# Weight low parts by a ScalarE pass and an accumulating DMA, in place of a GpSimd subtraction

## The chip, the cores and the metric

The kernel runs on one NeuronCore of a Trainium2 chip. The metric is the device time of one execution in microseconds. A core has five engines that run side by side and wait for each other by semaphores: TensorE (PE, matrix products), VectorE (DVE), ScalarE (ACT), GpSimd (POOL) and SyncE (SP, which here only issues transfers). The transfers of all queues run on the core's 16 DMA engines.

## The reference

A two-layer encoder over 256 frames of 2048 channels, in float32. Every sub-layer is `x <- x + norm_post(f(norm_pre(x)))` with root-mean-square norms. Layer 0's mixer projects the input to 3072 columns, pools one third over windows of 2 to 16 frames, sends the rest through a gate, a causal depthwise convolution of width 31, a layer norm and a swish, and projects back; layer 1's mixer is `y = W_out(B * conv3(C * h))` with B, C, h from one projection. Each mixer is followed by a dense MLP:

```python
def sq_relu_mlp(h, w1, w2):
    a = jax.nn.relu(jnp.einsum("btd,df->btf", h, w1))
    return jnp.einsum("btf,fd->btd", a * a, w2)
```

Nearly all of the arithmetic is products of the 256 frames with weight matrices that are read once.

## The kernel before, in words

**Products in three terms.** TensorE multiplies in a rounded float32 type (`F32R`). To keep float32's precision both factors are split in a high part (the value rounded) and a low part (the value minus its high part), and each product is made as high x high, high x low and low x high: L216, L217 and L218 in `mms`. The activations (`xh`/`xl`, `ah`/`al`, `yh`/`yl`) are the stationary factor and the weights (`whi`/`wlo`) the moving one; 256 frames are two row blocks `t`.

**The weight stream.** `specs` lists 722 weight slices in the order of their use, each 256 rows by 512 columns, in SBUF a tile of 128 partitions x 1024 numbers (512 KB). `prep_to(i)` (L166) prepares them up to slice i: SyncE loads the slice to a `raw` tile (L170), ScalarE rounds it to `whi` (L173), and an engine subtracts `whi` from `raw` to give `wlo` (L174). There are four `raw` buffers and nine of `whi` and of `wlo`. A load waits until the readers of the slice four before are done with their raw buffer; a rounding waits until TensorE is done with the slice nine before. `ahead` asks for slices up to eight beyond those that a block of products needs.

**Who subtracts.** VectorE does it for 633 slices. GpSimd does it for 89: the 62 slices 8 to 69 (from `lo_eng[0] = lambda i: pool` at L471 to L595, the stretch in which VectorE works through 31 x 8 convolution taps at L383 and L385), and nine slices at the start of each of `f1_0_0_0`, `sC0` and `f1_1_0_0` (L159 to L161), which are used right after a sub-layer ends.

**Boundaries of sub-layers.** `mix_close` (L558) forms the row scale of the sub-layer just done: ScalarE's square sums (L555 or L669) and root (L565), then VectorE's short chain L564, L289, L291, L292, L293 on one column per row. `close_row` adds the scaled block to the residual `x` (L319, 128x512 pieces). TensorE transposes `x` (L245), ScalarE rounds the transposed block (L231) and VectorE makes its low part (L234); only then can the next sub-layer's products start. Row scales of the pre-norm (L276, L287) follow later, since they are applied to the results.

**What sets the order.** Each engine executes its own list in order. The lists are made at build time by a scheduler that simulates the engines, so a change of one instruction can move others by some places.

Of the kernel before, what the change touches and what calls it, by code (L numbers as in the profile page):

```python
# [10 lines left out]
F32 = mybir.dt.float32  # L11
F32R = mybir.dt.float32r
BF16 = mybir.dt.bfloat16
AF = mybir.ActivationFunctionType
ALU = mybir.AluOpType
# [18 lines left out]
def trunk_kernel(  # L34
# [7 lines left out]
    pe, act, dve, pool = nc.tensor, nc.scalar, nc.vector, nc.gpsimd  # L42
# [14 lines left out]
    def nm(s):  # L57
        uid[0] += 1
        return f"{s}_{uid[0]}"

    def t512(shape=(P, CB), dt=F32):
        return tp.tile(list(shape), dt, tag="t512", name=nm("t"))

    def small(n=1):
        return sp.tile([P, n], F32, tag="sm", name=nm("sm"), padded_shape=[P, 4])
# [4 lines left out]
    def pst():  # L70
        return ps_t.tile([P, CB], F32, tag="t", name=nm("pt"))

# [1 line left out]
    xs = [cst.tile([P, D], F32, tag=f"x{t}", name=f"x{t}") for t in range(NT)]  # L74

    def load_x(t, c):
# [10 lines left out]
    par = cst.tile([P, 96 + 48 + 248], F32, tag="par", name="par")  # L87
    offs = {}

    def par_load(keyed, col, eng=pool):  # L90
        """Rows of 128 channels, one DMA per source, to be transposed to columns of par."""
        rows = t512()[:, :P]
        n = 0
        for key, v in keyed:
            offs.setdefault(key, col + n)
            eng.dma_start(rows[n : n + v.shape[0], :], v)
            n += v.shape[0]

        def tr():
            p = pst()  # L100
            pe.transpose(p[:, :n], rows[:n, :], ident[:n, :n])
            act.copy(par[:, col : col + n], p[:, :n])

        return tr
# [5 lines left out]
        o = offs[key] + i  # L110
        return par[:, o : o + 1]

# [1 line left out]
    specs = []  # L114

    def add_seg(w, k0, nk, c0):
# [42 lines left out]
    pool_lo = set()  # L159
# [3 lines left out]
    nxt = [0]  # L163
    lo_eng = [lambda i: dve]

    def prep_to(i):  # L166
        while nxt[0] <= min(i, len(specs) - 1):
            src, nj = specs[nxt[0]]
            raw = wp.tile([P, 2 * CB], F32, tag="raw", name=nm("raw"), bufs=4)
            nc.sync.dma_start(raw.rearrange("p (j n) -> p j n", j=nj), src)  # L170
            hi = wp.tile([P, 2 * CB], F32R, tag="whi", name=nm("whi"))
            lo = wp.tile([P, 2 * CB], F32R, tag="wlo", name=nm("wlo"))
            act.copy(hi, raw)  # L173
            (pool if nxt[0] in pool_lo else lo_eng[0](nxt[0])).tensor_tensor(lo, raw, hi.bitcast(F32), ALU.subtract)  # L174
            wt[nxt[0]] = (hi, lo)
            nxt[0] += 1

# [9 lines left out]
    tasks = []  # L187

    def later(d, fn):
        """Emit fn after d more slices of matrix products."""  # L190
        tasks.append([d, fn])

    def tick():
# [28 lines left out]
        n = len(ids)  # L222
        prep_to(ids[-1] + (AHEAD // 2 if t == 0 else AHEAD))

# [1 line left out]
    def split_cols(p, col0, dst, scale_cols):  # L226
        """PSUM bank of 4 transposed [128, 128] blocks, each times its column -> hi, lo."""
        hi, lo = dst
        for j in range(4):
            pj = p[:, j * P : (j + 1) * P]  # L230
            act.activation(hi[:, col0 + j, :], pj, AF.Copy, scale=scale_cols[j])  # L231
        for j in range(4):
            pj = p[:, j * P : (j + 1) * P]
            dve.scalar_tensor_tensor(  # L234
                lo[:, col0 + j, :], pj, scale_cols[j], hi[:, col0 + j, :].bitcast(F32),
                ALU.mult, ALU.subtract,
            )

    def split_plain(src, hi, lo):
        act.copy(hi, src)  # L240
        dve.tensor_tensor(lo, src, hi.bitcast(F32), ALU.subtract)  # L241
# [7 lines left out]
    def new_xT(t):  # L249
        for h in range(2):  # L250
            xT[t, h] = (
                xp.tile([P, 8, P], F32R, tag="xh", name=nm("xh")),
                xp.tile([P, 8, P], F32R, tag="xl", name=nm("xl")),
            )
# [7 lines left out]
    def norm_chunk(t, c, gkey, gbase):  # L262
        p = pst()
        transpose4(xs[t][:, c * CB : (c + 1) * CB], p)
        split_cols(p, 4 * (c % 2), xT[t, c // 2], [pcol(gkey, gbase + 4 * c + j) for j in range(4)])

    def sumsq(parts):
        s = small()
        dve.tensor_reduce(s, parts, mybir.AxisListType.X, ALU.add)
        return s  # L270
# [11 lines left out]
    def rsqrt(v, y=None, root=None):  # L282
        s = small()
        if root:
            root(s)
        else:
            act.activation(s, v, AF.Sqrt)  # L287
        y = y or small()
        dve.reciprocal(y, s)  # L289
        h = small()  # L290
        dve.scalar_tensor_tensor(h, y, v, y, ALU.mult, ALU.mult)  # L291
        dve.tensor_scalar(h, h, -0.5, 1.5, ALU.mult, ALU.add)  # L292
        dve.tensor_tensor(y, y, h, ALU.mult)  # L293
        return y
# [10 lines left out]
        return g  # L305

    def close_row(t, s, nxt_gain, final=False):
        """x += s * m, then the next sub-layer's transposed, gained, split input."""
        if not final:
            new_xT(t)  # L310
        for c in range(4):
            cs = slice(c * CB, (c + 1) * CB)
            if final and c == 0:
                for q in (slice(0, CB // 2), slice(CB // 2, CB)):
                    dve.scalar_tensor_tensor(xs[t][:, q], ms[t][:, q], s, xs[t][:, q],
                                             ALU.mult, ALU.add)
                    nc.sync.dma_start(out[t * P : (t + 1) * P, q], xs[t][:, q])
                continue
            dve.scalar_tensor_tensor(xs[t][:, cs], ms[t][:, cs], s, xs[t][:, cs], ALU.mult, ALU.add)  # L319
            if final:  # L320
                nc.sync.dma_start(out[t * P : (t + 1) * P, cs], xs[t][:, cs])
            else:
                later(2 + (c + 1) // 2, lambda c=c: norm_chunk(t, c, *nxt_gain))

# [1 line left out]
    for t in range(NT):  # L326
        new_xT(t)
    first = par_load((("mix_pre", chan_rows(mix_pre_g)),), 0, act)
# [37 lines left out]
    for i, tr in enumerate(rest):  # L366
        later(1 + i, tr)
# [42 lines left out]
            pwin.append(w)  # L410

    def pool_sum(g):
        """Windowed sums over time minus count times the frame, then / count."""
        ic = t512((P, T))
        nc.sync.dma_start(ic, inv_cnt[g * T : (g + 1) * T].partition_broadcast(P))
        p = pst()
        for c in range(2):
            ct = 2 * g + c
            o = p[:, c * T : (c + 1) * T]
            n = 0  # L420
            for s in range(2):
                for m in (uh[s], ul[s]):
                    pe.matmul(o, m[:, ct * P : (ct + 1) * P], pwin[s][:, g * T : (g + 1) * T],
                              start=n == 0, stop=n == 3)
                    n += 1
        pd = t512((P, 2, T))
        dve.tensor_tensor(
            pd, p.rearrange("p (c n) -> p c n", c=2),
            ic.unsqueeze(1).to_broadcast([P, 2, T]), ALU.mult,
        )  # L430
        ph = tp.tile([P, 2, T], F32R, tag="ph", name=nm("ph"), bufs=2)
        pl = tp.tile([P, 2, T], F32R, tag="pl", name=nm("pl"), bufs=2)
        split_plain(pd, ph, pl)
        pd_[g] = (ph, pl)
# [114 lines left out]
            split_plain(z, hi[:, :, tsl], lo[:, :, tsl])  # L549

    def mix_evac(t, cb, ps, gp, parts):
        """Mixer output block: square sums, and the block times the post-norm gain."""
        junk = tp.tile([P, CB], BF16, tag="junk", name=nm("junk"), bufs=2)
        i = nparts[t] = nparts.get(t, -1) + 1
        act.activation(junk, ps, AF.Square, accum_out=parts[t][:, i % 4 : i % 4 + 1])  # L555
        dve.tensor_tensor(ms[t][:, cb * CB : (cb + 1) * CB], ps, gp, ALU.mult)  # L556

    def mix_close(t, parts, nxt_gain, final=False):  # L558
        """Last block's square sum joins the others' on the way into the root."""
        base = small()  # L560
        dve.tensor_scalar(base, sumsq(parts[t][:, :3]), 1.0 / D, EPS, ALU.mult, ALU.add)
        last = parts[t][:, 3:4]
        v = small()
        dve.scalar_tensor_tensor(v, last, 1.0 / D, base, ALU.mult, ALU.add)  # L564
        r = rsqrt(v, root=lambda s: act.activation(s, last, AF.Sqrt, bias=base, scale=1.0 / D))  # L565
        close_row(t, r, nxt_gain, final)
# [47 lines left out]
        if cb == 1:  # L614
            mix_close(t, parts, ("ffn_pre", 0))

# [1 line left out]
    def ffn(l, nxt_gain, final=False):  # L618
        for t in range(NT):
            later(3 + t, lambda t=t: row_scale(t))  # L620
# [53 lines left out]

    ffn(0, ("mix_pre", KT))

# [1 line left out]
    for t in range(NT):  # L678
        later(3 + t, lambda t=t: row_scale(t))

# [107 lines left out]
```

## Time and profile before

| | |
|---|---|
| median of 3 runs | 2093.64 us (2092.41 to 2095.49) |
| the profiled execution: span from the first to the last instruction | 2096.0 us |
| busy: TensorE, VectorE, ScalarE, GpSimd | 2048.8, 1187.4, 1007.8, 221.5 us |
| of GpSimd's: the 89 subtractions | 214.3 us, 2.435 us each |
| VectorE's 633 subtractions | 775.4 us, 1.227 us each |
| ScalarE's 722 roundings | 760.1 us, 1.054 us each |
| transfers | 390.31 MB, 186 GB/s over the span |

The span is the profiled execution's own time as far as the profile gives it; what lies around it isn't shown. In the profile's lines a group reads: line, engine, operation, destination<-sources with shapes, count | busy us, mean ns of one | idle time of the engine just before, and what ended it. A wait reads: who <- whom: us in all, times, longest. Timelines give start and duration in us, and in brackets the idle time before.

### The profile page before, as it was taken

The numbers are of one execution on the slowest core, as the hardware profiler recorded it, in microseconds if no ns is written. First come the engines' busy times: TensorE is split into PE (matmuls) and PEld (weight loads), VectorE is DVE, ScalarE is ACT, GpSimd is POOL, SyncE is SP. The second block draws the span as 40 slices with busy tenths as digits, with TensorE's granted clock in tenths as the row PEclk, the third lists the DMA queues.
The fourth block names the chain that finished last, engine by engine and source line by source line (L and its number), as shares of the span: only waits on it lengthen the run. The fifth ranks groups of instructions, "written<-read, shape, count | busy, mean of one in ns | idle before, by whom it ended". The sixth has DMA issues, their size and how long they took to land.

```text
span 2096.0 us, 24559 instructions
## 1 busy us (share of the span) xinstructions
PE 2048.8 (98%) x9253; PEld 1693.0 (81%) x9253; DVE 1187.4 (57%) x1494; ACT 1007.8 (48%) x1296; POOL 221.5 (11%) x111
## 2 busy tenths in 40 slices
PE   8999889999999999999999999989999999999998
PEld 7888778888888888887788888878888888888886
DVE  4787765445454555546655655565455454454545
ACT  7454565445344354444643444465444444354443
POOL 5886210000000000002100000220000000000000
PEclk9999999999999999999999999999999999999999
DMA  7665445556565555555555565546556565565553
GB/s 259 197 208 174 151 161 191 190 171 206 196 196 171 196 186 196 189 173 170 174 199 180 182 204 181 191 156 212 180 178 211 174 201 186 175 202 199 192 170 120
DMA packets 203079, 390.31 MB, mean 186 GB/s; under 512 B 12368, under 2 KB 14512, under 8 KB 202960
## 3 DMA queue, kind: packets, MB, share of 16 engines
q1 hardware_dynamic: 202656, 388.55, 56.3%
q8 instruction: 72, 1.18, 0.2%
q14 instruction: 47, 0.39, 0.1%
q0 software_dynamic: 256, 0.18, 0.0%
q10 hardware_dynamic: 48, 0.02, 0.0%
HBM read 386.60 MB, written 2.10 MB: 185 GB/s over the span
## 4 chain that ended last, share of the span: by engine, by line
PE 84%; DVE 3%; DMA 1%; ACT 0%; issue 0%; DVEq 0%; SPq 0%; ACTq 0%
PE pg L218 27%; PE pg L216 27%; PE pg L217 27%; PE pt L245 2%; DVE x L319 1%; DVE sm L291 0%; DVE sm L293 0%; DMA gp<-in_mix_post_g_dram 0%; DMA raw<-in_ab_w_out_dram 0%; DVE sm L564 0%; DMA raw<-in_ffn_w_dram 0%; DMA raw<-in_sc_w_in_dram 0%; DVE m L556 0%; ACT whi L173 0%; DVE m L671 0%
## 5 line engine op out<-in xcount | busy, mean ns | idle before, releaser
L174 DVE TENSOR_TENSOR wlo<-raw,whi 128x1024 fp32r<-128x1024 f32 x633 | 775.4, 1227 | 583.9 <-ACT whi L173 550.3
L173 ACT CAST whi<-raw 128x1024 fp32r<-128x1024 f32 x722 | 760.1, 1054 | 581.8 <-PE pg L218 381.8
L218 PE MATMUL pg<-whi,xl 128*128 128x512 f32 x1568 | 618.5, 395 | 17.9 <-DVE xl L234 17.9
L216 PE MATMUL pg<-whi,xh 128*128 128x512 f32 x1568 | 612.6, 392 | 1.3 <-ACT xh L231 0.7
L217 PE MATMUL pg<-wlo,xh 128*128 128x512 f32 x1568 | 612.2, 391 | 0.0
L217 PE MATMUL pg<-wlo,ah 128*128 128x512 f32 x1024 | 399.2, 390 | 0.0
L216 PE MATMUL pg<-whi,ah 128*128 128x512 f32 x1024 | 398.7, 389 | 0.0
L218 PE MATMUL pg<-whi,al 128*128 128x512 f32 x1024 | 398.2, 391 | 0.0
L218 PEld LDWEIGHTS pg<-whi,xl 128*128 128x128 f32 x1568 | 295.8, 189 | 79.0 <-DVE xl L234 20.1
L217 PEld LDWEIGHTS pg<-wlo,xh 128*128 128x128 f32 x1568 | 295.8, 189 | 61.7
L216 PEld LDWEIGHTS pg<-whi,xh 128*128 128x128 f32 x1568 | 295.9, 189 | 61.1 <-ACT xh L231 1.7
L174 POOL TENSOR_TENSOR wlo<-raw,whi 128x1024 fp32r<-128x1024 f32 x89 | 214.3, 2435 | 1012.4 <-DVE wlo L174 693.8
L217 PEld LDWEIGHTS pg<-wlo,ah 128*128 128x128 f32 x1024 | 192.6, 188 | 40.2
L216 PEld LDWEIGHTS pg<-whi,ah 128*128 128x128 f32 x1024 | 192.6, 188 | 39.5
L218 PEld LDWEIGHTS pg<-whi,al 128*128 128x128 f32 x1024 | 192.5, 188 | 39.3
L634 ACT ACTIVATE t<-pg,rr 128x512 f32<-128x512 f32 x64 | 43.8, 685 | 190.6 <-PE pg L218 190.6
L664 DVE TENSOR_TENSOR m<-pg,m 128x512 f32<-128x512 f32 x112 | 76.9, 686 | 89.4 <-PE pg L218 89.4
L216 PE MATMUL pg<-whi,yh 128*128 128x512 f32 x256 | 101.2, 396 | 1.6 <-ACT yh L240 1.5
L217 PE MATMUL pg<-wlo,yh 128*128 128x512 f32 x256 | 100.9, 394 | 0.0
L218 PE MATMUL pg<-whi,yl 128*128 128x512 f32 x256 | 98.8, 391 | 0.2 <-DVE yl L241 0.2
L385 DVE SCALAR_TENSOR_TENSOR acc<-pp,par,acc 128x256 f32<-128x256 f32 x240 | 96.3, 479 | 0.1
L241 DVE TENSOR_TENSOR al<-pt,ah 128x512 fp32r<-128x512 f32 x64 | 44.0, 687 | 71.8 <-ACT ah L240 71.7
(124 smaller groups left out, 858.8 us busy)
## 6 DMA issues: line engine op xcount, KB each, us to landing
raw<-in_ffn_w_dram SPq DMA_DIRECT2D x512, 512.0 KB, 4.7
raw<-in_sc_w_in_dram SPq DMA_DIRECT2D x96, 512.0 KB, 4.8
raw<-in_ab_w_in_dram SPq DMA_DIRECT2D x48, 512.0 KB, 4.4
raw<-in_ab_w_out_dram SPq DMA_DIRECT2D x32, 512.0 KB, 3.9
raw<-in_sc_w_out_dram SPq DMA_DIRECT2D x32, 512.0 KB, 5.4
x<-in_x_dram SPq DMA_DIRECT2D x8, 256.0 KB, 7.7
gp<-in_mix_post_g_dram SPq DMA_DIRECT2D x8, 256.0 KB, 6.2
gp<-in_ffn_post_g_dram SPq DMA_DIRECT2D x8, 256.0 KB, 4.3
```

The lines of the kernel that those rows point to most:

```text
L173: act.copy(hi, raw)
L174: (pool if nxt[0] in pool_lo else lo_eng[0](nxt[0])).tensor_tensor(lo, raw, hi.bitcast(F32), ALU.subtract)
L216: pe.matmul(ps, lh, wh, start=start and k == 0, stop=False)
L217: pe.matmul(ps, lh, wl, start=False, stop=False)
L218: pe.matmul(ps, ll, wh, start=False, stop=stop and k == n - 1)
L241: dve.tensor_tensor(lo, src, hi.bitcast(F32), ALU.subtract)
L245: pe.transpose(p[:, j * P : (j + 1) * P], src[:, j * P : (j + 1) * P], ident)
L319: dve.scalar_tensor_tensor(xs[t][:, cs], ms[t][:, cs], s, xs[t][:, cs], ALU.mult, ALU.add)
L385: dve.scalar_tensor_tensor(a, src, wcol, a, ALU.mult, ALU.add)
L634: act.activation(rl, ps, AF.Relu, scale=rr[t])
L664: dve.tensor_tensor(dst, ps, dst, ALU.add)
```

## The change

For the 89 slices that GpSimd subtracted, ScalarE makes a second pass over the raw tile, `Copy` with the factor -1 into the `F32R` tile `wlo`, which gives minus the rounded weights; then GpSimd's queue issues a transfer that adds the raw tile to `wlo` in place (`accum_op`). The result is raw minus rounded, as before. TensorE's low-part products now wait for that transfer, and so does the load that reuses the raw buffer. The slices that VectorE subtracts are as they were. The change also empties some comment lines; all lines after L174 stand five lower in the new file.

```diff
             act.copy(hi, raw)
-            (pool if nxt[0] in pool_lo else lo_eng[0](nxt[0])).tensor_tensor(lo, raw, hi.bitcast(F32), ALU.subtract)
+            eng = pool if nxt[0] in pool_lo else lo_eng[0](nxt[0])
+            if eng is pool:
+                act.activation(lo, raw, AF.Copy, scale=-1.0)
+                pool.dma_start(lo, raw, accum_op=ALU.add)
+            else:
+                eng.tensor_tensor(lo, raw, hi.bitcast(F32), ALU.subtract)
             wt[nxt[0]] = (hi, lo)
```

ScalarE's list where the long GpSimd stretch begins (slices 8 and on), before and then after. Numbers in names count tiles and differ between the two.

```order
L231 ACTIVATE xh_99<-pt_306,par 128x128 x4
L173 CAST whi_427<-raw_425 128x1024
L173 CAST whi_433<-raw_431 128x1024
L173 CAST whi_439<-raw_437 128x1024
L231 ACTIVATE xh_103<-pt_319,par 128x128 x4
L173 CAST whi_445<-raw_443 128x1024
L102 COPY par<-pt_510 128x64
```
```order
L236 ACTIVATE xh_99<-pt_306,par 128x128 x4
L173 CAST whi_427<-raw_425 128x1024
L176 ACTIVATE wlo_428<-raw_425 128x1024
L173 CAST whi_434<-raw_432 128x1024
L176 ACTIVATE wlo_435<-raw_432 128x1024
L173 CAST whi_441<-raw_439 128x1024
L176 ACTIVATE wlo_442<-raw_439 128x1024
L236 ACTIVATE xh_103<-pt_319,par 128x128 x4
L173 CAST whi_448<-raw_446 128x1024
L176 ACTIVATE wlo_449<-raw_446 128x1024
L102 COPY par<-pt_522 128x64
```

Behind each rounding stands the second pass over the same raw tile, and the other work of ScalarE behind both.

SyncE's loads in the same stretch with the semaphores they wait for, before and then after. `Pool` is GpSimd, `Activation` ScalarE, `DMASW` a transfer that GpSimd issued, `DMAHW` one of SyncE's own.

```order
L170 DMA raw_455<-in_ab_w_in_dram 128x2x512 [waits DMAHW4_49,Pool_49]
L170 DMA raw_461<-in_ab_w_in_dram 128x2x512 [waits DMAHW5_49,Pool_49]
L170 DMA raw_467<-in_ab_w_in_dram 128x2x512 [waits DMAHW6_49,Pool_49]
L170 DMA raw_473<-in_ab_w_in_dram 128x2x512 [waits DMAHW7_49,Pool_49]
L170 DMA raw_479<-in_ab_w_in_dram 128x2x512 [waits DMAHW0_49,Pool_49]
```
```order
L170 DMA raw_460<-in_ab_w_in_dram 128x2x512 [waits DMAHW4_49,DMASW1_49,Activation_49]
L170 DMA raw_467<-in_ab_w_in_dram 128x2x512 [waits DMAHW5_49,DMASW2_49,Activation_49]
L170 DMA raw_474<-in_ab_w_in_dram 128x2x512 [waits DMAHW6_49,DMASW3_49,Activation_49]
L170 DMA raw_481<-in_ab_w_in_dram 128x2x512 [waits DMAHW7_49,DMASW4_49,Activation_49]
L170 DMA raw_488<-in_ab_w_in_dram 128x2x512 [waits DMAHW0_49,DMASW5_49,Activation_49]
```

A load waited for GpSimd's subtraction of the slice four before; now it waits for that slice's accumulating transfer to have landed.

ScalarE's list at the boundary after layer 0's mixer, before and then after, from the last square sums of the first row block to the rounding of its new activations.

```order
L555 ACTIVATE junk_2346,parts_2075<-opart_1807 128x512
L173 CAST whi_2304<-raw_2302 128x1024
L565 ACTIVATE sm_2355<-parts_2075,sm_2349 128x1
L173 CAST whi_2310<-raw_2308 128x1024
L173 CAST whi_2316<-raw_2314 128x1024
L173 CAST whi_2415<-raw_2413 128x1024
L555 ACTIVATE junk_2410,parts_2076<-opart_1810 128x512
L173 CAST whi_2421<-raw_2419 128x1024
L231 ACTIVATE xh_2363<-pt_2396,par 128x128 x4
```
```order
L176 ACTIVATE wlo_2368<-raw_2365 128x1024
L173 CAST whi_2367<-raw_2365 128x1024
L570 ACTIVATE sm_2421<-parts_2137,sm_2415 128x1
L176 ACTIVATE wlo_2375<-raw_2372 128x1024
L173 CAST whi_2374<-raw_2372 128x1024
L176 ACTIVATE wlo_2382<-raw_2379 128x1024
L173 CAST whi_2381<-raw_2379 128x1024
L176 ACTIVATE wlo_2482<-raw_2479 128x1024
L173 CAST whi_2481<-raw_2479 128x1024
L560 ACTIVATE junk_2476,parts_2138<-opart_1864 128x512
L173 CAST whi_2488<-raw_2486 128x1024
L176 ACTIVATE wlo_2489<-raw_2486 128x1024
```

Five second passes have come in among the roundings ahead of the new activations (L231, now L236), which follow directly behind the last row shown.

## The prediction

> **What bounds the kernel now.** The page comes first: its span line, and the shares of the chain that ended last, by engine and by line.
>
> ```profile
> span 2096.0 us, 24559 instructions
> PE 84%; DVE 3%; DMA 1%; ACT 0%; issue 0%; DVEq 0%; SPq 0%; ACTq 0%
> PE pg L218 27%; PE pg L216 27%; PE pg L217 27%; PE pt L245 2%; DVE x L319 1%; DVE sm L291 0%; DVE sm L293 0%; DMA gp<-in_mix_post_g_dram 0%; DMA raw<-in_ab_w_out_dram 0%; DVE sm L564 0%; DMA raw<-in_ffn_w_dram 0%; DMA raw<-in_sc_w_in_dram 0%; DVE m L556 0%; ACT whi L173 0%; DVE m L671 0%
> ```
>
> TensorE's three products per weight slice are the chain; a change elsewhere counts only where TensorE waits. So I looked next at busy time by stretches: the long stretch in which GpSimd makes the low parts (26 to 205), an ordinary stretch (280 to 972), and the three layer boundaries at which GpSimd takes nine slices each. Columns: length, then busy time and instruction count of TensorE, its weight loads, VectorE, ScalarE and GpSimd, granted clock, DMA share, GB/s.
>
> ```profile
> 26.00:205.00 179.00, 175.95 (x846) 147.15 (x845) 129.67 (x295) 92.68 (x118) 147.73 (x62) 0.99 0.63 198
> 243.00:280.00 37.00, 26.57 (x114) 21.02 (x113) 30.86 (x43) 18.71 (x43) 21.98 (x9) 0.93 0.55 169
> 280.00:972.00 692.00, 692.00 (x3114) 573.03 (x3114) 362.80 (x369) 329.36 (x385) 0.18 (x1) 1.00 0.57 187
> 972.00:1010.00 38.00, 29.39 (x124) 22.95 (x123) 27.98 (x41) 18.13 (x44) 21.64 (x10) 0.94 0.48 139
> 1340.00:1380.00 40.00, 32.72 (x146) 26.73 (x145) 30.37 (x47) 21.76 (x48) 22.94 (x9) 0.92 0.60 187
> ```
>
> In the long GpSimd stretch TensorE is busy 175.95 of 179 us, so there is almost nothing to win there and much to lose. At the boundaries it is idle 10.4, 8.6 and 7.3 us, 26.3 us together: that is all that the change can win in waits.
>
> What paces the long stretch: GpSimd's timeline (first and last entry), its group and ScalarE's rounding in the same stretch, and SyncE's longest wait.
>
> ```profile
> 28.86 40.26 POOL L174 TENSOR_TENSOR wlo<-raw,whi 128x1024 fp32r<-128x1024 f32 x17 [22.57 <-ACT whi L173]
> ...
> 195.34 7.08 POOL L174 TENSOR_TENSOR wlo<-raw,whi 128x1024 fp32r<-128x1024 f32 x3 [6.18 <-ACT whi L173]
> ```
> ```profile
> L174 POOL TENSOR_TENSOR wlo<-raw,whi 128x1024 fp32r<-128x1024 f32 x62 | 147.7, 2413 | 48.4 <-ACT whi L173 48.1
> L173 ACT CAST whi<-raw 128x1024 fp32r<-128x1024 f32 x64 | 67.3, 1053 | 64.9 <-DMA raw<-in_ab_w_in_dram 29.6 <-PE pg L218 25.1 <-DMA raw<-in_ab_w_out_dram 6.5
> ```
> ```profile
> SPq L170 <- POOL wlo L174: 133.5, 58, 8.1
> ```
>
> The 62 slices run from 28.86 to 202.42, so 173.6/62 = 2.80 us a slice. TensorE sets that: twelve products a slice at 692/3114 = 0.222 us are 2.67 us. The SyncE row shows the second limit close behind. A weight load goes into one of four raw buffers and waits until GpSimd is done with the slice four before.
>
> ```profile
> q1 hardware_dynamic: 18816, 35.19, 62.3%
> raw<-in_ab_w_in_dram SPq DMA_DIRECT2D x38, 512.0 KB, 4.4
> ```
>
> With a load landing 4.4 us after issue, 1.05 us of rounding and 2.41 us of subtraction a raw buffer is held 7.9 us. Four of them could deliver a slice every 2.0 us, well under 2.80.
>
> **The change, part by part.**
>
> *The long stretch, ScalarE.* Each slice gains an activation of the same 128x1024 shape from SBUF to SBUF as the rounding, so I price it at that row, 1.05 us. ScalarE's work without the 67.3 us of rounding is 92.68 - 67.3 = 25.4 us, 0.41 a slice; with two passes it is 2.5 us a slice. That fits in 2.80, barely, and the pass stands ahead of everything queued behind it on ScalarE (the sigmoids and copies that VectorE's convolution waits for). Alone it costs nothing, covered by TensorE's 2.67; the cover is 0.2 us thin.
>
> *The long stretch, the raw ring.* The subtraction (2.41 us) leaves the ring. The second pass, GpSimd's issue and the landing of an accumulating transfer enter it, and SyncE's load four slices later waits for all that. No accumulating transfer is in this trace. Its nearest rows are the 512 KB load above and GpSimd's own small transfers:
>
> ```profile
> L96 POOL DMA_DIRECT2D t<-in_conv_w_dram x2 | 1.1, 536 | 0.0
> ```
> ```profile
> t<-in_conv_w_dram POOLq DMA_DIRECT2D x2, 62.0 KB, 5.8
> ```
>
> Landing from below: like a load, 4.4 us. The ring is then 4.4 + 1.05 + 1.05 + 0.54 + 4.4 = 11.4 us, a quarter of it 2.86 a slice. From above: the 5.8 us of 62 KB plus the time of the other 450 KB. A 512 KB load occupies all 16 engines for 0.623 x 179/67 = 1.66 us (67 such loads in the stretch), so 450 KB take 1.5 us when moved once; an accumulation also reads its destination, so twice, 3.0. That gives 8.8 us, a ring of 15.8, a quarter of it 3.96. I take the upper one, because it comes from the same queue.
>
> *The long stretch, the DMA engines.* Per slice they have 1.66 us for the load. The accumulation moves as many bytes, and if the second read is free it costs 1.66 again, 3.32 in all. If it is not, 3.32 on top, 4.98 in all. Either is over 2.80, so the engines (62.3% busy now) become the bound or nearly so. The Trainium skill, "Collectives: The Full Stack", section "The bandwidth ceiling: the fold count and why AG ≠ RS ≠ AR", says that an add in the DMA path is slow not for the add but for its two source reads on one read ring, and gives a measured ratio of 1.93 to a copy. By it the sum would be 1.66 + 3.20 = 4.9 us a slice, +130 us; without it only the two ends above stand. No run so far shows which holds.
>
> I take 4.1 us a slice: a little over the ring's upper end (loads land later when the engines are fuller), and the middle of the two DMA ends (4.15). That is 62 x (4.1 - 2.80) = +81 us. Ends for this term: 62 x (2.86 - 2.80) = +4, and, with both landings doubled by contention, (2 x 4.4 + 2.1 + 0.54 + 2 x (4.4 + 1.66))/4 = 5.9 us a slice, +192.
>
> *The three boundaries.* Here GpSimd's subtraction does harm today. VectorE's timeline at the first one:
>
> ```profile
> 253.59 2.35 DVE L564 SCALAR_TENSOR_TENSOR sm<-parts,sm 128x1 f32<-128x1 f32 x1
> ...
> 256.05 2.22 DVE L291 SCALAR_TENSOR_TENSOR sm<-sm,sm 128x1 f32<-128x1 f32 x1
> ...
> 258.49 2.08 DVE L293 TENSOR_TENSOR sm<-sm,sm 128x1 f32<-128x1 f32 x1
> 260.60 2.74 DVE L319 SCALAR_TENSOR_TENSOR x<-m,sm,x 128x512 f32<-128x512 f32 x4
> ...
> 274.42 0.22 DVE L291 SCALAR_TENSOR_TENSOR sm<-sm,sm 128x1 f32<-128x1 f32 x1
> ```
> ```profile
> PE pt L245 <- DVE x L319: 4.2, 1, 4.2
> PE pg L218 <- DVE xl L234: 6.1, 2, 5.7
> ```
>
> A one-column instruction with two SBUF inputs takes 2.2 us while GpSimd subtracts and 0.22 us when it doesn't. Three of them in a row delay the residual update by 6 us, and TensorE waits 4.2 us for it. That goes away. What is late next is ScalarE: nine more passes (9 x 1.05 = 9.4 us) stand in its order between the square sums, the root and the rounding of the new activations (L231), and the slice whose rounding stands just ahead of L231 must wait for a raw buffer that an accumulation now holds some 5 us longer. The low parts themselves are covered by the nine pairs of weight buffers, up to eight slices ahead; without that cover nine slices at +1.3 us would cost 12 us a boundary. Ends: -26 us (all waits gone) and +28 (3 x 9.4 on the path). I take -8 in all: a third of the waits won net.
>
> *The rest.* The other 633 subtractions stay on VectorE; loads and products are the same ones, some a few places earlier or later: nothing.
>
> Sum: +81 - 8 = +73. The profiled execution's 2096.0 us is 2.4 us over the median of the runs, 2093.64; the difference is carried to the median: 2093.6 + 73, rounded to 2166 us.
>
> **The rivals.**
>
> *Hidden, and faster.* If an accumulation lands within 4.2 us of its issue, the ring stays at 11.2 us, four slices at TensorE's rate, and the long stretch costs only about +4. The boundaries then return most of their waits, say 20 of 26.3: 2093.6 + 4 - 20 = 2078. For it: loads land in 4.4 us at 63% DMA share, and VectorE's slow instructions are plain in the timeline. Against it: both DMA sums are over 2.80 us a slice. If the boundaries return less, this case ends within 0.2% of before.
>
> *Accumulation one packet at a time.* If each row's read, add and write must finish before the next, or the two streams slow each other, both landings double: 5.9 us a slice, +192 - 8, 2278 us. It decides as soon as an accumulation takes over 12 us to land. The trace has no row for or against it.
>
> *TensorE loses its clock.* After a wait of 5.7 us the products run at half rate. The chain of waits shows the step of one product before and after:
>
> ```profile
> 229.12 0.23 PE pg L217
> ...
> 280.76 0.43 PE pg L217
> ```
>
> If starvation comes in lumps (four raw buffers landing together, then a gap over some 4 us), twelve products at 0.43 take 5.1 us, and the slice costs that instead of 4.1: 62 x 2.3 - 8 = +135, 2228 us. Against it: waits of 1.3 us a slice are shorter than any that lowered the clock here, and the boundary stretches still show 0.92 to 0.94. The Trainium skill, "TensorE: Matmul & The Clock Gate", section "What's actually happening", puts the drop after an idle window of about 3.4 us; by that rule spread waits leave the clock alone and lumped ones halve it, and the two boundary waits above (4.2 and 5.7 us) agree with it.
>
> **How the numbers follow.** Forecast (ring and DMA at about 4.1 us) 0.64; hidden and faster 0.13; one packet at a time 0.14; clock lost 0.09. A measurement of this kernel can tell about 0.2%, 4 us, from no change. Faster by more than that: 0.09, the larger part of the second case. Within it: 0.05, the rest of that case and the forecast's lowest end. Slower: 0.86. The range starts at 2093.6 + 4 = 2098, the ring's low end with nothing won at the boundaries, and ends at 2280, which takes in the serial case at its worked price and leaves out what is worse than it.
>
> **What would show it.** In the profile after: in the stretch that held the 62 slices, TensorE's busy share falls from 98% to about 70%, with its waits at the product that reads the accumulated low part, and SyncE's put down to the accumulating transfer; the DMA share there rises over 0.9; the accumulating transfers show about 9 us from issue to landing; GpSimd's busy time almost vanishes; L291, L293 and L564 take 0.2 us at all boundaries. The prediction is wrong if the stretch still ends near 205 us, or if the landing is under 5 us. It is wrong in its cause if the landing is short and ScalarE or a lower TensorE clock holds the stretch.

## The result, and the profile after

The changed kernel takes 2172.72 us, median of four runs (2169.04 to 2177.02); the kernel before, beside it, 2094.29 (2092.41 to 2095.49). The ratio is 1.0374, with a 95% interval of 1.0356 to 1.0391. The forecast was 2166. One profile used below, that of the plain copy, is of an execution 1% over that kernel's median, with a granted TensorE clock of 0.927 where its other runs had 0.995 to 0.997.

The page of the kernel after, its span and the chain that ended last by engine:

```profile
span 2168.3 us, 24729 instructions
PE 81%; DMA 13%; issue 4%; ACT 2%; DVE 1%; POOL 0%; POOLq 0%; DVEq 0%; SPq 0%; ACTq 0%
```

DMA was 1% of the chain and is now 13%. The stretches of the kernel after follow, with columns as in the prediction: the long stretch, then 40 us or a little more of each of the three boundaries.

```profile
30.00:290.00 260.00, 207.03 (x874) 158.37 (x872) 130.08 (x314) 151.09 (x180) 53.58 (x62) 0.94 1.03 251
318.00:358.00 40.00, 31.03 (x138) 24.81 (x137) 18.30 (x49) 27.21 (x57) 7.75 (x9) 0.87 0.93 226
1044.00:1084.00 40.00, 31.23 (x137) 24.96 (x136) 18.03 (x49) 25.86 (x56) 7.97 (x11) 0.87 0.92 225
1413.00:1455.00 42.00, 34.69 (x152) 27.98 (x151) 15.83 (x47) 28.11 (x59) 7.75 (x9) 0.92 0.93 226
```

In the long stretch the DMA share went from 0.63 to 1.03 (a share adds up packet times; as it passes 1, some of them overlap, so a little over 1 is read as full), and TensorE is busy 80% of it where it was 98%. At the boundaries the share is 0.92 and more, where it was 0.48 to 0.60.

GpSimd's timeline gives the pace: the issue of the first and of the 62nd accumulation.

```profile
30.10 0.95 POOL L177 DMA_DIRECT2D wlo<-raw  x1 [23.76 <-DVE rr L298]
...
287.40 0.91 POOL L177 DMA_DIRECT2D wlo<-raw  x1 [2.08 <-ACT wlo L176]
```

That is (287.40 - 30.10) / 61 = 4.22 us a slice, against 2.80 before. The DMA queues of the same stretch (packets, MB, share of the 16 engines) and the landings of the two kinds of transfer:

```profile
q1 hardware_dynamic: 17789, 33.22, 36.3%
q0 software_dynamic: 8782, 31.99, 66.0%
...
raw<-in_ab_w_in_dram SPq DMA_DIRECT2D x36, 512.0 KB, 6.3
wlo<-raw POOLq DMA_DIRECT2D x62, 512.0 KB, 7.7
```

The accumulations (q0) take 0.66 x 260 / 62 = 2.8 us of all 16 engines each. The loads take 0.363 x 260 / 62 = 1.5. Together that is 4.3 us a slice, the pace. With the share near 1 this sum has to equal the pace, so it does not yet say that the engines set it; the experiments do. Who waits in that stretch, first TensorE's longest entry, then SyncE's:

```profile
PE pg L222 <- DMA wlo<-raw: 34.6, 27, 3.6
```
```profile
SPq L170 <- DMA wlo<-raw: 219.6, 59, 8.3
```

TensorE waits at the product that reads the accumulated low part, and SyncE's loads wait for a raw buffer that an accumulation holds. The second row alone would make the raw ring (the four raw buffers in turn) the bound; the experiments say otherwise.

At the first boundary, VectorE's closing chain and ScalarE's list up to the new activations:

```profile
326.25 0.15 DVE L569 SCALAR_TENSOR_TENSOR sm<-parts,sm 128x1 f32<-128x1 f32 x1
...
327.57 0.22 DVE L296 SCALAR_TENSOR_TENSOR sm<-sm,sm 128x1 f32<-128x1 f32 x1
...
328.01 0.16 DVE L298 TENSOR_TENSOR sm<-sm,sm 128x1 f32<-128x1 f32 x1
```
```profile
342.15 1.04 ACT L173 CAST whi<-raw 128x1024 fp32r<-128x1024 f32 x1 [8.51 <-DMA raw<-in_ffn_w_dram]
343.10 1.05 ACT L176 ACTIVATE wlo<-raw 128x1024 fp32r<-128x1024 f32 x1
344.06 2.15 ACT L236 ACTIVATE xh<-pt,par 128x128 fp32r<-128x128 f32 x8
```

VectorE's three instructions fell from about 2.2 to 0.2 us, as forecast. In their place ScalarE stands 8.51 us, waiting for the raw tile of a slice whose rounding is ahead of L236 in its list.

Where the time came from: GpSimd starts the first boundary's slices at 243.97 us before and at 318.38 after, 74.4 later. The ends of the two executions are 72.3 us apart. So the long stretch holds the whole loss; the 2 us between the two numbers, which would be the boundaries' gain, are less than the spread of the runs (2169.04 to 2177.02). The medians are 78 us apart; the profiled executions differ from theirs by 2 to 3 us, one up and one down. Of the 72.3 us TensorE idles 49.8 (97.0 after, 47.2 before); in the other 22.5 it is busy longer with the same 9253 products, which run slower, as read below under *Clock lost*.

### The profile page after: what moved, and what is told of

Same layout as the page of the kernel before. It is cut to its first block, busy times and chain, and to the rows that moved or that the text cites. A ratio compares the mean times of both kernels' runs of the same rounds, so it can differ in the third digit from the quotient of the medians.

```text
span 2168.3 us, 24729 instructions
## 1 busy us (share of the span) xinstructions
PE 2071.3 (96%) x9253; PEld 1698.9 (78%) x9253; DVE 1137.5 (52%) x1494; ACT 1086.7 (50%) x1385; POOL 84.0 (4%) x111
## 4 chain that ended last, share of the span: by engine, by line
PE 81%; DMA 13%; issue 4%; ACT 2%; DVE 1%; POOL 0%; POOLq 0%; DVEq 0%; SPq 0%; ACTq 0%
PE pg L222 26%; PE pg L223 26%; PE pg L221 26%; DMA wlo<-raw 4%; DMA raw<-in_ab_w_in_dram 3%; DMA raw<-in_ab_w_out_dram 2%; PE pt L250 2%; DMA raw<-in_ffn_w_dram 1%; ACT whi L173 1%; DMA raw<-in_sc_w_in_dram 0%; ACT wlo L176 0%; DMA raw<-in_pool_w_dram 0%; DVE wlo L179 0%; DMA t<-in_mix_pre_g_dram 0%; ACT junk L281 0%
## 5 line engine op out<-in xcount | busy, mean ns | idle before, releaser
L222 PE MATMUL pg<-wlo,xh 128*128 128x512 f32 x1568 | 620.1, 396 | 30.7 <-DMA wlo<-raw 30.6
L221 PE MATMUL pg<-whi,xh 128*128 128x512 f32 x1568 | 617.1, 395 | 25.1 <-ACT xh L236 17.7
L177 POOL DMA_DIRECT2D wlo<-raw x89 | 76.8, 863 | 1233.9 <-ACT wlo L176 1110.7
L176 ACT ACTIVATE wlo<-raw 128x1024 fp32r<-128x1024 f32 x89 | 94.3, 1060 | 1.0 <-DMA raw<-in_ffn_w_dram 0.9
```

Of the source, the lines that this page charges most:

```text
L176: act.activation(lo, raw, AF.Copy, scale=-1.0)
L177: pool.dma_start(lo, raw, accum_op=ALU.add)
L221: pe.matmul(ps, lh, wh, start=start and k == 0, stop=False)
L222: pe.matmul(ps, lh, wl, start=False, stop=False)
```

## The experiments

Two theories for the long stretch. D: the time of the 16 DMA engines bounds it. R: the ring of four raw buffers does, each held until the accumulation has landed. For the boundaries: the full DMA engines, or a held raw buffer, give back what VectorE's faster chain wins. Diffs are against the kernel after unless said.

### Six raw buffers in the changed kernel

```diff
-    wp = ctx.enter_context(tc.tile_pool(name="wp", bufs=9))
+    wp = ctx.enter_context(tc.tile_pool(name="wp", bufs=8))
-            raw = wp.tile([P, 2 * CB], F32, tag="raw", name=nm("raw"), bufs=4)
+            raw = wp.tile([P, 2 * CB], F32, tag="raw", name=nm("raw"), bufs=6)
```

The raw tiles of `load_pool`, from the same buffers, get the same `bufs=6`; eight pairs of high and low parts instead of nine make the room.

> The changed kernel with six raw buffers instead of four (and eight instead of nine of the high and of the low parts, which makes the room). Theory D (the DMA engines' time is the bound: 1.6 us for a load plus 2.85 us for an accumulation is over 4 us a slice, at a share of 1.03): the 62 slices still come at 4.1 to 4.3 us each, the landings of loads and accumulations grow by about half, in all 2150 to 2180 us. Theory R (the ring of four raw buffers is the bound: load 6.3, two passes 2.1, issue 0.9, landing 7.7 make 17 us, a quarter is 4.2): with six buffers a sixth is 2.8 us a slice, TensorE's rate, and the whole takes 2085 to 2110 us. At the boundaries both expect ScalarE's wait for a raw tile (8.5 us now) to go.

Measured: 2154.15 us, ratio to the kernel before 1.0286 (1.0270 to 1.0302). The long stretch in its windows:

```profile
29.00:268.00 239.00, 202.65 (x871) 160.50 (x870) 129.56 (x314) 150.05 (x182) 53.51 (x62) 0.92 1.05 270
```

The 62 issues run from 28.97 to 266.22 us, 3.89 us a slice. The share stays full, and the landings grew: 8.9 us for an accumulation, 10.9 for a load. Two more buffers mostly lengthened the queue. D holds in the whole (2154 of 2150 to 2180), and R is 44 us off; but the pace is under D's 4.1 to 4.3, so the ring was worth 0.33 us a slice. At the boundaries both theories were wrong: ScalarE's wait for a raw tile is about halved (up to 4.4 us), not gone, and TensorE waits 24.6 us for new activations in all, where it was 17.7.

### A plain copy in place of the accumulation

```diff
-                pool.dma_start(lo, raw, accum_op=ALU.add)
+                pool.dma_start(lo, raw)
```

> The 89 transfers copy the raw tile over the low part instead of adding to it; the low parts are then wrong, so this is for the time alone. Theory D with a second read that costs: a copy takes about 1.6 us of the engines where the accumulation took 2.85, a slice 3.1 to 3.4 us, in all 2105 to 2130 us. Theory D with a free second read (the add or the conversion is what costs): still 4.2 us a slice, 2165 to 2180 us. Theory R: landing shorter by 1 to 2 us, a ring of about 15 to 16 us, 3.8 to 4.0 us a slice, 2145 to 2160 us.

Measured: 2094.10 us, ratio 1.0005 (0.9984 to 1.0027), no change, and some 11 us less than the lowest number that any theory gave, that of D with a second read that costs; whether the boundaries win that back is open. GpSimd's queue over the whole execution, of the kernel after and then of the copy:

```profile
q0 software_dynamic: 13072, 46.85, 11.7%
```
```profile
q0 software_dynamic: 13072, 46.85, 6.4%
```

The same packets and bytes: 0.117 x 2168.3 / 89 = 2.85 us of the engines for an accumulation, 0.064 x 2112.8 / 89 = 1.52 for a copy, a ratio of 1.88. A load and a copy are then about 3.0 us a slice, close to TensorE's 2.80. The copy's long stretch (by this window alone, 0.95 x 209 / 62 = 3.2 us a slice):

```profile
30.00:239.00 209.00, 203.30 (x871) 155.64 (x870) 129.44 (x312) 151.18 (x180) 32.84 (x62) 0.84 0.95 315
```

TensorE is busy 97% of it, at a DMA share of 0.95 (and a clock of 0.84). The kind of transfer, not the transfer as such, costs the time. The copy writes the same `F32R` tile from the same raw tile, so the types are not what costs; the run does not separate the second read from the add.

### ScalarE's pass without any transfer

```diff
-                pool.dma_start(lo, raw, accum_op=ALU.add)
```

> ScalarE's second pass stays, the 89 transfers are left out; the low parts are then minus the rounded weights, so this is for the time alone. Theories D and R alike: the second pass costs nothing in the long stretch (2.5 us a slice on ScalarE against 2.8 on TensorE), the stretch takes what it took before, and at the boundaries VectorE's short instructions take 0.2 us and no raw tile is held, so 15 to 25 us are won there: 2068 to 2080 us. Rival S (ScalarE's passes are what holds the long stretch or the boundaries): 2095 us or more.

Measured: 2074.58 us, ratio 0.9907 (0.9891 to 0.9923). Its long stretch and first boundary:

```profile
28.00:200.00 172.00, 169.67 (x800) 140.71 (x799) 116.94 (x287) 141.42 (x171) 0.00 (x0) 0.99 0.62 202
```
```profile
243.00:283.00 40.00, 37.41 (x170) 30.14 (x169) 20.46 (x60) 31.19 (x68) 0.00 (x0) 0.96 0.53 171
```

TensorE is busy 169.67 of 172 us, so the second pass is hidden. At the boundary it idles 2.6 us where it idled 10.4, and in all three together 6.6 where it idled 26.3. GpSimd's subtraction costs the kernel before 20 us in all; the 89 transfers cost 2172.7 - 2074.6 = 98.

### Only the 27 boundary slices accumulate

```diff
-            if eng is pool:
+            if nxt[0] in pool_lo:
```

> Only the 27 slices at the three boundaries take the second pass and the accumulation; GpSimd subtracts in the long stretch as before. By the two traces (differences to before of 72.3, 71.1 and 72.3 us at the second and third boundary and at the end) the boundaries won and lost about as much: 2090 to 2097 us. Rival: with the weight stream not late at the first boundary, VectorE's freed chain shows, 2070 to 2088 us.

Measured: 2093.96 us, ratio 0.9997 (0.9987 to 1.0007), no change. The first boundary in the kernel before and in this one:

```profile
243.00:283.00 40.00, 29.57 (x121) 23.34 (x120) 33.03 (x50) 18.71 (x43) 21.98 (x9) 0.90 0.53 166
```
```profile
243.00:283.00 40.00, 32.95 (x148) 26.35 (x147) 18.98 (x58) 29.29 (x65) 7.45 (x9) 0.91 0.97 246
```

TensorE's idle time here fell from 10.4 to 7.1 us, VectorE's busy time by 14, and the DMA share rose from 0.53 to 0.97. Its one wait left in this window is 7.1 us for ScalarE's new activations. Over the three boundaries it idles 24.6 us against 26.3: the 20 us that lie here are given back.

### Accumulating from HBM, all 89 slices

```diff
-                pool.dma_start(lo, raw, accum_op=ALU.add)
+                pool.dma_start(lo.rearrange("p (j n) -> p j n", j=nj), src, accum_op=ALU.add)
```

> The changed kernel, but the accumulating transfer reads its slice once more from HBM instead of from the raw tile; a raw buffer is then free after ScalarE's two passes. Theory D (the DMA engines' time is the bound): the 62 slices still come at about 4.2 us each, since the engines move as much; only the boundaries win, 2145 to 2165 us. Theory R (the raw ring is the bound): the ring shrinks to about 8.5 us, a quarter is 2.1 us, the stretch goes back to TensorE's 2.8 us a slice, in all 2070 to 2085 us.

Measured: 2160.73 us, ratio 1.0310 (1.0296 to 1.0325). The long stretch, and SyncE's longest wait in it:

```profile
30.00:286.00 256.00, 201.74 (x882) 155.75 (x880) 135.81 (x319) 158.62 (x188) 74.65 (x62) 0.97 1.10 263
```
```profile
SPq L170 <- ACT wlo L176: 114.7, 53, 4.0
```

The raw tile is now free as soon as ScalarE has read it, and no load waits for an accumulation. The pace is still (272.98 - 29.70) / 61 = 3.99 us and the engines are full. R falls: the 219.6 us that SyncE waited in the kernel after came mostly from full engines, as seen from a ring. Without the ring 0.23 us a slice come back.

### The boundaries alone, from HBM

The edits of the last two together, 27 slices.

> Second pass and accumulation from HBM in the 27 slices at the boundaries only; GpSimd subtracts in the long stretch as before. Theory H (at the boundaries the accumulation gives back what VectorE's freed chain wins, because it holds raw buffers and ScalarE waits for the next raw tile ahead of the new activations): ScalarE's wait of over 8 us there goes, 2073 to 2084 us. Rival (the engines being full is what gives it back: loads land late whatever holds the buffers): 2090 to 2096 us.

Measured: 2093.15 us, ratio 0.9990 (0.9980 to 0.9999), within 0.2%. The first boundary's window and TensorE's waits in it:

```profile
243.00:283.00 40.00, 34.03 (x145) 26.50 (x144) 18.68 (x53) 27.88 (x59) 10.94 (x9) 0.91 1.04 253
```
```profile
PE pg L222 <- DMA wlo<-in_ffn_w_dram: 3.9, 3, 2.4
PE pg L221 <- ACT xh L236: 1.7, 1, 1.7
```

The wait for the new activations shrank to 1.7 us, and waits for late low parts took its place: nine loads here land in 14.1 us (median), nine accumulations in 12.8. So a held buffer is not needed for the loss: with none held, the loads and accumulations of the full engines land late instead.

### The boundaries alone, from the raw tile, six raw buffers

The 27-slice edit and the buffer edit together.

> Accumulation from the raw tile in the 27 boundary slices only, with six raw buffers (and eight instead of nine of the high and of the low parts). Theory H: the load that ScalarE waited for finds a free buffer, 2075 to 2088 us. Rival (full engines): 2090 to 2098 us.

Measured: 2105.85 us, ratio 1.0050 (1.0038 to 1.0063): slower by 12 us, which neither theory expected. ScalarE's timeline at the first boundary:

```profile
257.75 1.04 ACT L176 ACTIVATE wlo<-raw 128x1024 fp32r<-128x1024 f32 x1
...
268.36 1.03 ACT L173 CAST whi<-raw 128x1024 fp32r<-128x1024 f32 x1
...
274.18 1.04 ACT L173 CAST whi<-raw 128x1024 fp32r<-128x1024 f32 x1 [4.17 <-DMA raw<-in_ffn_w_dram]
...
276.09 2.16 ACT L236 ACTIVATE xh<-pt,par 128x128 fp32r<-128x128 f32 x8
```

ScalarE runs twelve weight passes from 257.75 to 269.4 us and still waits 4.17 us for a raw tile ahead of L236. In the whole kernel TensorE waits 24.5 us for new activations, and 15.8 with four buffers. More buffers seem to let more passes stand ahead of the activations; that this is the 12 us was not tried by itself.

### The kernel before with six raw buffers

The buffer edit on the kernel before.

> The kernel before with six raw buffers and eight of the high and of the low parts, no accumulation: what the buffers alone do. Expected no change, 2090 to 2098 us: the raw ring of 7.9 us for four was far under TensorE's pace. Rival: eight pairs instead of nine cost lead at the boundaries, 2098 to 2110 us.

Measured: 2094.06 us, ratio 0.9995 (0.9986 to 1.0004), no change. In the kernel before, the buffers by themselves neither help nor harm.

### Only the 62 slices of the long stretch accumulate

```diff
-            if eng is pool:
+            if eng is pool and nxt[0] not in pool_lo:
```

> Only the 62 slices of the long stretch accumulate; the 27 at the boundaries stay GpSimd's subtraction. If the long stretch alone carries the loss and the boundaries' gain and loss cancel, as the boundaries alone gave no change: 2172 us, within 5 us of the full change, TensorE waiting at the boundaries as before the change (10, 9 and 7 us idle, VectorE's one-column instructions at 2.2 us again). Rival: if in the full change the boundaries were won because the DMA engines are emptier there than it seemed, this is about 20 us slower than the full change, 2190.

Measured: 2170.49 us, ratio 1.0357 (1.0340 to 1.0375), 1.5 us from the expectation. Its long stretch and first boundary:

```profile
30.00:292.00 262.00, 207.74 (x879) 157.32 (x878) 131.26 (x314) 153.08 (x182) 53.27 (x62) 0.95 1.03 252
316.00:356.00 40.00, 31.46 (x126) 24.92 (x125) 32.77 (x49) 18.69 (x43) 22.02 (x9) 0.85 0.53 166
```

The long stretch by itself is the whole loss, 2170.5 - 2094.4 = 76 us. The rival (20 us slower than the full change) is not there.

### Every second slice of the long stretch accumulates

```diff
-            if eng is pool:
+            if eng is pool and nxt[0] not in pool_lo and nxt[0] % 2:
```

> Of the 62 slices only every second accumulates, the others and the boundaries stay GpSimd's subtraction. If the 16 DMA engines' time is the bound in the long stretch, two slices need two loads and one accumulation, 2 x 1.5 to 1.66 + 2.8 = 5.8 to 6.1 us against 5.6 of TensorE: 2.9 to 3.05 us a slice, +6 to +15 us, 2100 to 2109, with a DMA share near 0.95 in the stretch. Rival: if each accumulation puts its own delay on the path (a wait of TensorE for each low part, whatever the engines' load), half of them cost half of the loss, +39, 2133.

Measured: 2130.19 us, ratio 1.0171 (1.0157 to 1.0185). Theory D's 2100 to 2109 missed by over 20 us; the number is the rival's. Its window, TensorE's longest wait and the queues:

```profile
30.00:240.00 210.00, 189.74 (x849) 154.67 (x848) 123.89 (x298) 118.67 (x144) 99.38 (x62) 0.93 0.92 241
```
```profile
PE pg L222 <- DMA wlo<-raw: 10.0, 6, 3.2
```
```profile
q1 hardware_dynamic: 18359, 34.32, 51.0%
q0 software_dynamic: 4464, 16.25, 40.9%
```

The rival's row is not there: TensorE waits for 6 of 31 accumulations, 10 us, not for each. An accumulation still takes 0.409 x 210 / 31 = 2.8 us of the engines, and all transfers 0.92 x 210 / 62 = 3.1 us a slice, a little over the expected end; the pace is (230.98 - 28.40) / 61 = 3.32. So the price of one accumulation holds at a share under 1 too, but it explains only 0.3 of the 0.5 us that a slice became slower. What fills the last 0.2 us is open. A share of 0.92 by itself does not: the plain copy kept TensorE busy 97% of the time at 0.95. The raw ring and GpSimd's list, in which a subtraction now stands behind an accumulation's issue, were not tried here.

### Four of nine boundary slices, from the raw tile and from HBM

```diff
+    pool_mid = set()
+    for key in ("f1_0_0_0", "sC0", "f1_1_0_0"):
+        pool_mid |= set(range(seg[key][0] + 3, seg[key][0] + 7))
-            if eng is pool:
+            if nxt[0] in pool_mid:
```

> Long stretch as before the change. At each boundary only four of the nine slices (the fourth to the seventh, those whose subtraction runs beside VectorE's closing chain) accumulate from the raw tile, the other five stay GpSimd's subtraction. If the loss at the boundaries comes from full DMA engines, four accumulations are 11 us of them instead of 25 in some 40 us: the share stays at about 0.75, VectorE's chain still runs at 0.2 us, and half or more of the 20 us is won: 2080 to 2086. Rival: the held raw buffer ahead of the new activations alone costs it, however few accumulate: 2094, no change.

> As the run with four of nine slices, but the accumulation reads the slice from HBM instead of the raw tile, so no raw buffer is held. If full engines were the cause at the boundaries: 2080 to 2086, like the run from the raw tile. If the held raw buffer alone was: here 2076 to 2082 and there no change.

Measured: from the raw tile 2078.86 us, ratio 0.9930 (0.9917 to 0.9943), faster than both kernels; from HBM 2086.84, ratio 0.9963 (0.9950 to 0.9977). The boundaries of the first:

```profile
241.00:281.00 40.00, 36.36 (x163) 28.97 (x162) 28.05 (x63) 26.60 (x65) 16.14 (x9) 0.96 0.80 221
961.00:1001.00 40.00, 36.10 (x168) 28.88 (x167) 26.99 (x64) 28.05 (x67) 15.45 (x11) 1.00 0.78 219
1325.00:1365.00 40.00, 33.70 (x150) 26.80 (x149) 19.92 (x52) 24.58 (x56) 16.16 (x9) 0.91 0.75 208
```

TensorE idles 3.6, 3.9 and 6.3 us, 13.8 together, where it idled 26.3; the DMA share stays at 0.75 to 0.80. SyncE's loads still wait for accumulations (7.8 us in four waits at the first boundary), and the gain came. So the rival, by which a held buffer costs it however few accumulate, falls. One part of the expectation failed. VectorE's timeline at the first boundary (lines three lower than in the kernel after):

```profile
248.36 0.16 DVE L572 SCALAR_TENSOR_TENSOR sm<-parts,sm 128x1 f32<-128x1 f32 x1
...
249.70 2.07 DVE L299 SCALAR_TENSOR_TENSOR sm<-sm,sm 128x1 f32<-128x1 f32 x1
...
251.99 2.14 DVE L301 TENSOR_TENSOR sm<-sm,sm 128x1 f32<-128x1 f32 x1
```

Two of the three instructions are still slow, since the second and third subtraction ran just then; the gain came all the same. From HBM the gain was half, not equal. The issue rows at the third boundary, of the first and then of the second:

```profile
wlo<-raw POOLq DMA_DIRECT2D x4, 512.0 KB, 8.7
```
```profile
wlo<-in_ffn_w_dram POOLq DMA_DIRECT2D x4, 512.0 KB, 13.3
```

The slice's second journey from HBM lands 4.6 us later, and TensorE there waits 5.4 us for low parts. But its waits do not make the difference: over the whole kernel TensorE idles 33.8 us in the first (span 2076.2, busy 2042.4) and 35.2 in the second (2085.1, 2049.9). The other 7.5 of the 8.9 us are slower products: the granted clock around the three boundaries (59, 60 and 65 us) is 0.97, 1.00 and 0.95 in the first and 0.94, 0.94 and 0.92 in the second. Why it fell further there is not shown.

## Why the prediction was right

**The long stretch.** Forecast 4.1 us a slice and +81; measured 4.22, and 74 to 76 us at the end. 62 x 1.42 is 88. The rest is lead, as TensorE's products (the count in the first brackets) show, from the start to where the last of the 62 subtractions ended, in the kernel before, and to where the last accumulation was issued, in the kernel after:

```profile
0.00:202.42 202.42, 193.22 (x915) 160.40 (x916) 142.10 (x327) 113.61 (x168) 153.16 (x79) 0.99 0.66 211
```
```profile
0.00:287.40 287.40, 229.33 (x975) 176.44 (x976) 145.96 (x353) 174.46 (x237) 58.13 (x78) 0.95 1.01 255
```

TensorE had executed 915 products there before and 975 after. Slices were ready ahead of it before and just in time after; 60 products at 0.222 us are 13 us. The forecast had no term for this lead.

**The limit.** The forecast put the ring's upper end beside the middle of the two DMA ends and let them agree. That the engines would fill and set the pace was argued, and right: they are the bound (full with six buffers and with none held). That 4.1 came so near 4.22 is partly luck, since no row stood behind the middle of two ends of which neither held. The sum was helped too: 7 us too little for the pace, 13 too much for the missing lead and 8 that the boundaries did not give leave +75, beside a forecast of +73 and 78 between the medians. An accumulation takes 2.8 us of the engines, between the 1.66 and 3.32 that the ends assumed, and a load 1.5. The ring was worth 0.2 to 0.3 us a slice. In the kernel after it adds up to the same (6.3 + 1.05 + 1.05 + 0.86 + 7.7 = 17.0, a quarter 4.24) because full engines lengthen its landings; with six buffers these grew to 8.9 and 10.9 us.

The Trainium skill, "Collectives: The Full Stack", section "The bandwidth ceiling: the fold count and why AG ≠ RS ≠ AR", gives a measured ratio of 1.93 between a collective that copies and one that adds, and puts it to the add's two source reads. The 1.88 measured here, outside any collective, is close to it; that the second read is the reason is not shown here. The forecast's sum of 4.9 us a slice by that ratio was too high mainly because it took 1.66 us for the first transfer where 1.5 was measured.

**ScalarE's pass.** Forecast hidden, with 0.2 us to spare: without the transfers TensorE stays busy 169.67 of 172 us.

**The boundaries.** Forecast -8: "a third of the waits won net". This is the step that was off: measured none for the 27 slices alone (ratio 0.9997), and nothing clear of the spread within the full change (2172.72 us, and 2170.49 without them). The parts were as named: VectorE's chain freed, ScalarE then late for a raw tile. But the forecast priced that as one held buffer. It is the DMA engines, filled to 0.92 and more by nine accumulations in 40 us: with the buffer freed another wait came, without the transfers the whole 20 us came, and with four accumulations about 16 of them.

**The signs.** The share over 0.9, the waits at the low-part product and behind the accumulation, and VectorE's three instructions at 0.15 to 0.22 us at all boundaries came as forecast. Three sizes did not. TensorE's busy share is 80%, not about 70%, since its products ran slower (at 0.208 us each, as before, the 874 of the stretch would fill 70%). The landing is 7.7 us, not about 9. GpSimd is still busy 84.0 us, because the issue of an accumulation takes 0.86 us where the forecast took 0.54 from small transfers.

**The rivals.** *Hidden* needed a landing within 4.2 us; it was 7.7. *One packet at a time* needed over 12. *Clock lost* came in part: the granted clock is 0.94 in the long stretch, and a product takes 207.03 / 874 = 0.237 us on average where it took 175.95 / 846 = 0.208, not 0.43 throughout. TensorE still idles 53 of the 260 us, so this is taken to hide behind the DMA engines; no run tries it by itself. The Trainium skill, "TensorE: Matmul & The Clock Gate", section "What's actually happening", puts the half rate after an idle window of about 3.4 us. If that window is read as one wait, as the forecast did, this trace does not agree. The waits for low parts are 1.3 us on average (34.6 / 27) and 3.6 at most, one wait for ScalarE is 5.2, and half rate also came where the last two waits had been 1.85 and 1.80 us. A product and the clock of the next 3 us:

```profile
195.01 0.61 PE L222 MATMUL pg<-wlo,xh 128*128 128x512 f32 x1 [1.80 <-DMA wlo<-raw]
```
```profile
195.00:198.00 3.00, 2.99 (x8) 0.54 1.02 230
```

The second row has only TensorE's columns, the clock, the DMA share and GB/s. The kernel before shows it too: after a wait of 2.48 us at 169.06 the clock is 0.50 from 170 to 172. So the forecast's spread waits of 1.3 us were not as safe as it took them to be.

## What to carry to other kernels

Price an accumulating DMA as time of all 16 engines (here 2.8 us for 512 KB, nearly two copies) and add it to the loads of the same stretch; when the sum passes the compute time per tile, more buffers or another source change little (here they won back 19 and 12 of 78 us). A row that says "the load waits for its buffer" can be the echo of full engines: lengthen the ring or free the buffer and see whether the pace moves. The sum is a floor and not the whole forecast: with every second slice accumulating it explained 0.3 of the 0.5 us that a slice became slower. Where a substitute is good but its resource is small, use it for only as many tiles as the resource has room for: four of nine gained 0.7% where nine of nine gained nothing.

## What the runs showed of the hardware

- An accumulation costs 1.88 times the DMA engine time of a copy of the same packets (2.85 and 1.52 us for 512 KB, SBUF to SBUF), and 0.86 us of GpSimd to issue.
- Read from HBM, it lands later: 13.3 us where one from SBUF took 8.7 (third boundary, four of nine), and takes 1.20 us of GpSimd to issue.
- GpSimd's subtraction slows VectorE's one-column instructions with two SBUF inputs about tenfold (2.2 against 0.22 us); those with one input, between them at the first boundary, stay at 0.15 us. With nothing in its place the kernel ends 20 us earlier, though its 214 us of GpSimd time lie beside other work.
- A DMA share alone does not tell whether TensorE is fed: at 0.92 with 31 accumulations it was busy 90% of the stretch, at 0.95 with 62 copies 97% (at a clock of 0.84).
- TensorE's clock can halve without one long wait: 0.54 over 3 us behind waits of 1.85 and 1.80 us.
